# A hybrid attention and retention layer: a second pause in the index search, and later splits of the attention projection's weights

## The chip, the cores and the metric

The kernel runs on one core of one Trainium2 chip. The metric is the device time of one execution in microseconds (us); lower is better. Before the change it is 1831.25 us, the median of three runs (1830.81 to 1835.08). The engines are TensorE (PE), VectorE (DVE), ScalarE (ACT), GpSimd (POOL) and SyncE (SP), whose queue issues the DMAs.

## The reference

One decoder layer over a sequence of 1024 tokens, with model width 1024. What matters here:

```python
proj = jnp.dot(h, w_in)      # q, k, v; index q, k, w; retention q, k, v, g; two gates
# index scores: which keys a query may see
s_h = jnp.einsum('bqhd,bsd->bqhs', iqb, ikf) * idx_scale
score = jnp.einsum('bqh,bqhs->bqs', iwb * w_scale, jax.nn.relu(s_h))
score = jnp.where(causal[None], score, NEG)
_, idx = lax.top_k(score, topk)                  # topk = 256
# attention over the chosen keys, then
y_a = jnp.dot(att.reshape(B, S, N_HEADS_A * HEAD_DIM_A), w_attn_proj)
y_r = jnp.dot(jax.nn.silu(gr) * _head_groupnorm(ret, gn_w), w_ret_proj)
merged = jax.nn.sigmoid(ga) * y_a + jax.nn.sigmoid(gb) * y_r
x = x + gate1 * jnp.dot(merged, w_out)           # then a SwiGLU feed-forward and a norm
```

## The kernel before, in words

All matrix products of weights are done in three parts: a weight is split into a rounded part `hi` and a remainder `lo`, so is the activation, and hi·hi, hi·lo and lo·hi are summed in a bank of PSUM. The split of a weight (`split_weight`, L70, and `split_block`, L704) is one copy on ACT and one subtraction on POOL.

The stages that matter follow each other on PE like this:

1. Projections, index scores and retention (to about 490 us).
2. **Gated projections** (`run`, from L996): the remaining columns of `w_in`, multiplied by a Strassen-Winograd scheme with seven products for a 2x2 block (`Stream`, L708). For each product DVE may form a sum of weight blocks (`factor`, L739 and L743, into `wraw`), ACT and POOL split it (L706, L707), PE multiplies it (L771 to L775), ACT copies a result out of PSUM (L754) or DVE adds to one (L757, into `kept`, `sums`, `spare`).
3. **Retention tiles** (`make_g`, L932): eight tiles for each half of the tokens are transposed, gated on DVE (L936) and split (hi on ACT, L938; lo on DVE, L939).
4. **Retention projection** (from L996): y_r for eight column blocks `nt`. The first three are done half by half, with the last eight `make_g` between them; blocks 3 to 7 take both halves at once in two PSUM banks. DVE multiplies each result by its gate (`y_r_store`, L988, `sgr`).
5. **Attention** (from L1115): four pairs of heads `p`, eight blocks of 128 queries `qb`, two heads `e`, so 64 tiles. For each tile PE makes the logits (`lga`), DVE adds the mask and takes the maximum, ACT takes the exponential (L1060, `sx`), POOL scales (L1062), PE transposes (`tra`, three tiles behind the logits), ACT or DVE copies the result (`pt`, L1077, L1079), and PE multiplies with the values (`pva`). Blocks 2 to 7 of the queries use the finished index scores as the mask.
6. **Attention projection** (from L1162), its eight weight slots loaded and split by `cols_slot` (L101), and then the output projection, whose weights POOL multiplies by a gate (L1257) before they are split.

The **index search** (`select_all`, L436) finds for each query the 256th largest score by bisection on the bits of the float. For each bit from 30 to 0 DVE counts, in each of six score blocks (384 to 1024 columns), how many scores lie above the candidate (L450, a compare that also accumulates), then two tiny steps set the bit (L455, L470). A last count and five steps a block (L478 to L482) turn the scores into a mask. All of it is DVE work, issued with a late priority, so that the scheduler puts it between the other instructions. A scheduler sets the order in each engine's queue when the program is built; at run time each engine takes its queue strictly in that order. `turns_after` adds a dependency that only orders two instructions in one queue. With one, bit 8's first count stands behind the last split of the token sums in stage 2 (`paused[0]`).

PSUM has eight banks. In stages 2 to 4 they are three `mm`, two `tr` and three `lg`. Buffers for raw weights `wraw` are four by the time of the attention projection's loads: load 5 needs the buffer that the split of load 1 frees, and so on, and the loads of the output projection follow in the same ring.

Of the kernel before, what the change touches and what calls it, by code (L numbers as in the profile page):

```python
# [14 lines left out]
AF = mybir.ActivationFunctionType  # L15
# [4 lines left out]
P = 128  # L20
# [4 lines left out]
H = 512  # L25
HD = 64
# [17 lines left out]
def tile_hybrid_layer(ctx: ExitStack, tc: tile.TileContext, x, c, w_ada, b_ada, norm1_w, w_in,  # L44
                      w_attn_proj, w_ret_proj, gn_w, w_out, norm2_w, w_ffn_gate, w_ffn_up,
                      w_ffn_down, final_norm_w, rope_r, rope_a, rope_c, ret_mask, ret_scale, causal, out):
    nc = tc.nc
# [17 lines left out]
    def f32(ap):  # L65
        return ap.bitcast(F32)

    RING = 11

    def split_weight(raw, n, order=None, home=None):  # L70
        if home is not None:
            hi, lo = home[:, 0], home[:, 1]
        else:
            hi = ring.tile([P, H], R, name="whi", tag="whi", bufs=RING)
            lo = ring.tile([P, H], R, name="wlo", tag="wlo", bufs=RING)
        if order is None:
            nc.scalar.activation(hi[:, :n], raw[:, :n], AF.Copy)  # L77
            nc.gpsimd.tensor_sub(lo[:, :n], raw[:, :n], f32(hi[:, :n]))  # L78
        else:
            raw, hv, lv = order(raw, hi, lo)  # L80
            nc.scalar.activation(hv, raw, AF.Copy)
            nc.gpsimd.tensor_sub(lv, raw, f32(hv))
        return hi, lo
# [14 lines left out]
            nc.gpsimd.tensor_mul(raw[:, :n], raw[:, :n], scale)  # L98
        return split_weight(raw, n)

    def cols_slot(w, kt0, c0):  # L101

        raw = raw_tile()
        nc.sync.dma_start(
            out=raw.rearrange("p (k n) -> p k n", k=4),
            in_=w[kt0 * P:(kt0 + 4) * P, c0:c0 + P].rearrange("(k p) n -> p k n", p=P))
        return split_weight(raw, H)

    def mm_tok(ps, lhs, slots, n=H, ks=None):

# [11 lines left out]
    def turns_after(ins, other):  # L122

        tc.add_manual_dep(ins.ins, other.ins.name, NOSYNC, reason="order")
# [75 lines left out]
    def ps_mm():  # L200
        return psx.tile([P, H], F32, name="mm", tag="mm", bufs=3)
# [4 lines left out]
    def ps_lg():  # L206
        return psx.tile([P, H], F32, name="lg", tag="lg", bufs=3)
# [216 lines left out]
        last_score[0] = nc.vector.tensor_add(sc[:, W - P:W], sc[:, W - P:W], cm01[:, P:2 * P])  # L424

    last_score = [None]
    PAUSE = 8
    paused = []

    def all_scores():  # L430
# [5 lines left out]
    def select_all():  # L436

        tc.cur_priority += LATE
        n = len(score)
        cand, rej = (early.tile([P, 8], I32, name=x)[:, :n] for x in ("cand", "rej"))
        cnt, need = (early.tile([P, 8], F32, name=x)[:, :n] for x in ("cnt", "need"))
        eq = early.tile([P, S], U8, name="eq")
        rank = early.tile([P, S], I16, name="rank")
        at = [cand.bitcast(F32)[:, j:j + 1] for j in range(n)]

        def count(op, thr):
            ins = [nc.vector.tensor_scalar(eq[:, :sc.shape[1]], sc, thr[j], None, op0=op, op1=ALU.add,  # L450
                                           accum_out=cnt[:, j:j + 1]) for j, sc in enumerate(score)]
            return ins[0]

        def rejected(value):
            nc.vector.tensor_scalar(rej, cnt, float(TOPK), float(value), op0=ALU.is_lt, op1=ALU.mult)  # L455


        for j, sc in enumerate(score):
            ins = nc.vector.tensor_scalar(eq[:, :sc.shape[1]], sc, 0.0, None, op0=ALU.is_ge, op1=ALU.add,
                                          accum_out=cnt[:, j:j + 1])  # L460
            tc.add_manual_dep(ins.ins, last_score[0].ins.name, NOSYNC, reason="scores first")
        rejected(-1)
        nc.vector.tensor_scalar(cand, rej, 1 << 30, None, op0=ALU.bitwise_xor)
        for bit in range(30, -1, -1):
            first = count(ALU.is_ge, at)
            if bit == PAUSE:
                paused.append(first)
            rejected(1 << bit)
            if bit:
                nc.vector.scalar_tensor_tensor(cand, cand, 1 << (bit - 1), rej, op0=ALU.bitwise_xor,  # L470
                                               op1=ALU.bitwise_xor)
            else:
                nc.vector.tensor_tensor(cand, cand, rej, op=ALU.bitwise_xor)
        count(ALU.is_gt, at)
        nc.vector.tensor_scalar(need, cnt, -1.0, float(TOPK), op0=ALU.mult, op1=ALU.add)
        for j, sc in enumerate(score):
            e, r = eq[:, :sc.shape[1]], rank[:, :sc.shape[1]]
            nc.vector.tensor_scalar(e, sc, at[j], None, op0=ALU.is_equal)  # L478
            nc.vector.tensor_tensor_scan(r, e, e, 0.0, op0=ALU.add, op1=ALU.max)
            nc.vector.scalar_tensor_tensor(e, r, need[:, j:j + 1], e, op0=ALU.is_gt, op1=ALU.mult)  # L480
            nc.vector.tensor_scalar(sc, sc, at[j], NEG, op0=ALU.is_lt, op1=ALU.mult)
            nc.vector.scalar_tensor_tensor(sc, e, NEG, sc, op0=ALU.mult, op1=ALU.add)  # L482
        tc.cur_priority -= LATE
# [6 lines left out]
    for t in range(NT):  # L490
        ps = ps_mm()
        for k in range(KT):
            n = 5 * (KT * t + k) // 4 - 8
# [5 lines left out]
        st = projp.tile([P, H], F32, name="vst", bufs=2)  # L499
# [432 lines left out]
    def make_g(k, hf, rt, sg):  # L932
        tp = ps_tr()
        for i in range(4):
            nc.tensor.transpose(tp[:, i * P:(i + 1) * P], rt[:, i * P:(i + 1) * P], ident)
        nc.vector.scalar_tensor_tensor(sg, tp, colT[:, 72 + k:73 + k], sg, op0=ALU.mult, op1=ALU.mult)  # L936
        hi = gT.hi[hf][:, k, :]
        nc.scalar.activation(hi, sg, AF.Copy)  # L938
        nc.vector.tensor_sub(gT.lo[hf][:, k, :], sg, f32(hi))  # L939


    seq = [(st, m) for m in ORDER for st in flow[:2]]
# [54 lines left out]
    for hf in range(2):  # L997
        for nt in range(NF):
            slots, sg = first[nt]
            ps = ps_mm()  # L1000
            mm_ch([ps], gT, slots, (hf,))
            y_r_store(hf, ps, sg)
            if hf == 0:
                for k in ((0, 1, 2), (3, 4, 5), (6, 7))[nt]:
                    make_g(k, 1, *staged[k])
            else:
                nc.sync.dma_start(out=m_d[nt], in_=sg)
    st_s.close()
    pre = pool("pre", side="left", stack=mid)
    for nt in range(NF, KT):  # L1010
        slots, sg = y_r_open(nt)
        pss = [ps_mm(), ps_mm()]
        mm_ch(pss, gT, slots)
        for hf in range(2):
            y_r_store(hf, pss[hf], sg)
        nc.sync.dma_start(out=m_d[nt], in_=sg)
        if nt in (4, 5):
            make_stack(nt - 4, pre)
# [15 lines left out]
        nc.sync.dma_start(out=v, in_=v_d[:, :, p * P:(p + 1) * P])  # L1034
        return v

    def att_logits(qb, st):
        qs, kh, kl = st
        W = (qb + 1) * P
        sx = att.tile([P, S], F32, name="sx", bufs=6)  # L1040
        mx = att.tile([P, 16], F32, name="mx", bufs=6)
        if qb < 2:
            bias = cm01[:, P:2 * P] if qb == 0 else cm01
        else:
            bias = score[qb - 2]
        chunks = {1: (256,), 2: (256,), 3: (384,), 4: (512,), 5: (384, 256), 6: (512, 256), 7: (512, 384),
                  8: (512, 512)}[qb + 1]
        c0 = 0
        for i, n in enumerate(chunks):
            lg = psa.tile([P, H], F32, name="lga", bufs=4)  # L1050
            nc.tensor.matmul(lg[:, :n], lhsT=qs[:, qb * P:(qb + 1) * P], rhs=kh[:, c0:c0 + n], start=True, stop=False)
            nc.tensor.matmul(lg[:, :n], lhsT=qs[:, qb * P:(qb + 1) * P], rhs=kl[:, c0:c0 + n], start=False, stop=True)
            n = min(n, W)
            nc.vector.tensor_tensor_reduce(
                out=sx[:, c0:c0 + n], in0=lg[:, :n], in1=bias[:, c0:c0 + n], op0=ALU.add, op1=ALU.max, scale=1.0,
                scalar=-3e38 if i == 0 else mx[:, i - 1:i], accum_out=mx[:, i:i + 1])
            c0 += n
        top = mx[:, len(chunks) - 1:len(chunks)]
        nc.vector.tensor_scalar(mx[:, 2:3], top, -(HD ** -0.5), None, op0=ALU.mult)
        nc.scalar.activation(sx[:, :W], sx[:, :W], AF.Exp, scale=HD ** -0.5, bias=mx[:, 2:3], accum_out=mx[:, 3:4])  # L1060
        nc.vector.reciprocal(mx[:, 3:4], mx[:, 3:4])  # L1061
        nc.gpsimd.tensor_scalar(sx[:, :W], sx[:, :W], mx[:, 3:4], 1.0, op0=ALU.mult, op1=ALU.mult)  # L1062
        return sx
# [51 lines left out]
    for p in range(4):  # L1115
        for qb in range(NT):
            for e in range(2):
                sx = att_logits(qb, stacks[2 * p + e])
                todo_t.append((p, qb, e, sx))
                drain(3, 1)  # L1120
            if p < 3 and qb == 0:
                v_sb[p + 1] = load_v(p + 1)
                for h in (2 * p + 2, 2 * p + 3):
                    make_stack(h, pre if p == 1 else att)
# [35 lines left out]

    sg5 = slab_tile(6, [P, 4, S], F32, "sg5")
    for nt in range(KT):  # L1162
        slot = cols_slot(w_attn_proj, 0, nt * P)
        sg = sg5[:, nt % 4, :]
        nc.sync.dma_start(out=sg, in_=sga_d[nt])
        for hf in range(2):
# [481 lines left out]
```

## Time and profile before

| what | value |
|---|---|
| median of three runs | 1831.25 us |
| the profiled execution's own time | 1836.64 us |
| its span, first to last instruction | 1834.9 us |
| PE busy | 1712.6 us (93%) |
| DVE busy | 1222.0 us (67%) |
| POOL busy | 937.4 us (51%) |
| ACT busy | 739.8 us (40%) |
| mean granted TensorE clock | 0.982 |
| DMA | 266.49 MB, mean 145 GB/s |

The profile is of one execution. Its page gives busy shares and groups of instructions by source line; its trace can be asked for stretches of time, for waits (who waited for whom, by semaphores), and for single instructions in order of time. A wait is put down to the instruction that came last, even where that one was itself only held up by another. Some matmul records are missing, so counts of matmuls are a little low.

### The profile page before, as it was taken

The page shows a single profiled execution, that of the slowest core. Times are in us where ns is not written, and L with a number is a line of the kernel's source. Part 1 is how long each engine was busy: PE and PEld are TensorE (multiplying, and loading weights), DVE is VectorE, ACT ScalarE, POOL GpSimd, SP SyncE. Part 2 cuts the span into 40 slices and gives each one's busy share as a digit, 9 for nine tenths or more (in the row PEclk, how much of TensorE's full clock was granted, in tenths as well). Part 3 has the DMA queues.
Part 4 walks back from the last instruction along what each step waited for, and adds up shares of the span by engine and source line. Part 5 has one row for each costly group of instructions (what it writes and reads, how often), then busy time and mean ns, then how long its engine had stood idle before and what let it go on. Part 6 is the DMA issues. An engine that isn't in the chain of part 4 may idle for free. (4 is left out here: it accounts for less than half of the span.)

```text
span 1834.9 us, 24613 instructions
## 1 busy us (share of the span) xinstructions
PE 1712.6 (93%) x8266; PEld 1399.1 (76%) x8266; DVE 1222.0 (67%) x2088; ACT 739.8 (40%) x1448; POOL 937.4 (51%) x902
## 2 busy tenths in 40 slices
PE   5899989999989979999989999889998999999998
PEld 3788868878768758788767888677776788788887
DVE  7637599999699995441557547765666555377565
ACT  3525532432443324430567235443332333355444
POOL 4571293773553669530454634444444444466564
PEclk9999999999989999999989999999999999999999
DMA  8530245433323335874851730134666333287663
GB/s 287 162 83 34 75 138 172 136 94 115 110 81 115 107 104 194 251 217 143 204 141 49 230 136 24 53 97 165 231 218 244 113 120 98 94 262 233 188 177 113
DMA packets 184703, 266.49 MB, mean 145 GB/s; under 512 B 13872, under 2 KB 113664, under 8 KB 182144
## 3 DMA queue, kind: packets, MB, share of 16 engines
q1 hardware_dynamic: 184576, 264.91, 46.3%
q8 instruction: 65, 1.06, 0.3%
q14 instruction: 62, 0.51, 0.1%
HBM read 195.39 MB, written 69.47 MB: 144 GB/s over the span
## 5 line engine op out<-in xcount | busy, mean ns | idle before, releaser
L707 POOL TENSOR_TENSOR flo<-tmp,fhi 128x512 fp32r<-128x512 f32 x88 | 129.2, 1470 | 157.5 <-ACT fhi L706 127.6
L78 POOL TENSOR_TENSOR wlo<-wraw,whi 128x512 fp32r<-128x512 f32 (+2 forms) x116 | 142.3, 1239 | 104.7 <-ACT whi L77 99.3
L450 DVE TENSOR_SCALAR_CACHE_REDUCE eq<-score,cand 128x384 uint8<-128x384 f32 (+2 forms) x192 | 180.7, 941 | 4.2
L116 PE MATMUL mm<-whi,hT_hi 128*128 128x512 f32 (+1 forms) x432 | 162.5, 379 | 2.3 <-ACT qk L611 1.8
L119 PE MATMUL mm<-whi,hT_lo 128*128 128x512 f32 (+1 forms) x432 | 163.2, 379 | 0.0
L118 PE MATMUL mm<-wlo,hT_hi 128*128 128x512 f32 (+1 forms) x432 | 162.8, 377 | 0.0
L771 PE MATMUL ya<-hc,fhi 128*128 128x512 f32 x336 | 134.8, 402 | 14.9 <-DVE c L757 13.5
L1496 DVE TENSOR_TENSOR dslot<-draw,dslot 128x512 fp32r<-128x512 f32 x88 | 93.8, 1093 | 70.6 <-ACT dslot L1495 62.4
L773 PE MATMUL ya<-hc,fhi 128*128 128x512 f32 x336 | 134.0, 399 | 5.2 <-DVE hc L1415 5.2
L775 PE MATMUL ya<-hc,flo 128*128 128x512 f32 x336 | 132.3, 398 | 0.0
L1495 ACT ACTIVATE dslot<-draw 128x512 fp32r<-128x512 f32 x154 | 90.2, 626 | 97.1 <-PE ya L1514 37.3
L1496 POOL TENSOR_TENSOR dslot<-draw,dslot 128x512 fp32r<-128x512 f32 x66 | 97.4, 1485 | 62.1 <-ACT dslot L1495 59.4
L77 ACT ACTIVATE whi<-wraw 128x512 fp32r<-128x512 f32 (+2 forms) x116 | 66.9, 591 | 129.6 <-DMA wraw<-in_w_in_dram 53.1
L707 POOL TENSOR_TENSOR flo<-raws,fhi 128x512 fp32r<-128x512 f32 x58 | 80.7, 1392 | 73.8 <-ACT fhi L706 57.0
L771 PE MATMUL yb<-hc,fhi 128*128 128x512 f32 x248 | 97.8, 395 | 5.5 <-ACT hc L1414 3.7
L706 ACT ACTIVATE fhi<-tmp 128x512 fp32r<-128x512 f32 x88 | 55.3, 632 | 117.4 <-PE ya L773 72.7
L775 PE MATMUL yb<-hc,flo 128*128 128x512 f32 x248 | 96.8, 391 | 3.2 <-POOL flo L707 3.2
L707 POOL TENSOR_TENSOR wlo<-wraw,whi 128x512 fp32r<-128x512 f32 x52 | 83.6, 1615 | 30.9 <-ACT whi L706 25.1
L773 PE MATMUL yb<-hc,fhi 128*128 128x512 f32 x248 | 96.8, 390 | 1.8 <-DVE hc L1415 1.7
L1062 POOL TENSOR_SCALAR sx<-sx,mx 128x1024 f32<-128x1024 f32 (+7 forms) x64 | 47.4, 748 | 98.7 <-DVE mx L1061 74.1
L116 PEld LDWEIGHTS mm<-whi,hT_hi 128*128 128x128 f32 x432 | 82.2, 191 | 14.5 <-ACT qk L611 2.2
L119 PEld LDWEIGHTS mm<-whi,hT_lo 128*128 128x128 f32 x432 | 82.3, 191 | 12.7
(400 smaller groups left out, 4951.1 us busy)
## 6 DMA issues: line engine op xcount, KB each, us to landing
draw<-act_d SPq DMA_DIRECT2D x77, 256.0 KB
mw<-in_w_ada_dram SPq DMA_DIRECT2D x32, 512.0 KB
act_d<-c SPq DMA_DIRECT2D x62, 256.0 KB
raw<-in_w_in_dram SPq DMA_DIRECT2D x26, 512.0 KB
raws<-in_w_ffn_gate_dram SPq DMA_DIRECT2D x24, 512.0 KB
raws<-in_w_ffn_up_dram SPq DMA_DIRECT2D x24, 512.0 KB
dw<-in_w_ffn_down_dram SPq DMA_DIRECT2D x22, 512.0 KB
dw_d<-dw SPq DMA_DIRECT2D x11, 1024.0 KB
```

Of the source, the lines that this page charges most:

```text
L77: nc.scalar.activation(hi[:, :n], raw[:, :n], AF.Copy)
L78: nc.gpsimd.tensor_sub(lo[:, :n], raw[:, :n], f32(hi[:, :n]))
L116: ins = nc.tensor.matmul(ps, lhsT=ahi, rhs=whi[:, :n], start=(i == 0), stop=False)
L118: nc.tensor.matmul(ps, lhsT=ahi, rhs=wlo[:, :n], start=False, stop=False)
L119: nc.tensor.matmul(ps, lhsT=alo, rhs=whi[:, :n], start=False, stop=(i == last))
L450: ins = [nc.vector.tensor_scalar(eq[:, :sc.shape[1]], sc, thr[j], None, op0=op, op1=ALU.add, accum_out=cnt[:, j:j + 1]) for j, sc in enume ...
L707: nc.gpsimd.tensor_sub(lo, src, f32(hi))
L771: mm = nc.tensor.matmul(ps, lhsT=whi[:, k, :], rhs=hhi[:, k, :], start=first, stop=False, skip_group_check=True)
L773: nc.tensor.matmul(ps, lhsT=whi[:, k, :], rhs=hlo[:, k, :], start=False, stop=False, skip_group_check=True)
L775: nc.tensor.matmul(ps, lhsT=wlo[:, k, :], rhs=hhi[:, k, :], start=False, stop=last, skip_group_check=True)
L1495: nc.scalar.activation(slot[:, 0], raw, AF.Copy)
L1496: lo_eng.tensor_sub(slot[:, 1], raw, f32(slot[:, 0]))
```

## The change

Four edits:

- The search gets a second pause: the first count of bit 3 must stand behind `made`, the last `gT_lo` of stage 3. `make_g` now returns that instruction. Bits 3 to 0, the final count and the masks move behind it.
- In the retention projection blocks 3 to 7 use one `mm` and one `lg` bank each, where they used two `mm`.
- The ACT half of the split of the attention projection's weight `nt` must stand behind the exponential of the second head in pair `2 + nt // 4`, query block `2 * (nt % 4)`.
- `att_logits` takes `p`, to note the exponentials under `exps[p, qb]`.

```diff
-    def split_weight(raw, n, order=None, home=None):
+    def split_weight(raw, n, order=None, home=None, behind=None):
...
-            nc.scalar.activation(hi[:, :n], raw[:, :n], AF.Copy)
+            ins = nc.scalar.activation(hi[:, :n], raw[:, :n], AF.Copy)
+            if behind is not None:
+                turns_after(ins, behind)
             nc.gpsimd.tensor_sub(lo[:, :n], raw[:, :n], f32(hi[:, :n]))
...
-    PAUSE = 8
+    PAUSES = (8, 3)
...
-            if bit == PAUSE:
+            if bit in PAUSES:
                 paused.append(first)
...
-        nc.vector.tensor_sub(gT.lo[hf][:, k, :], sg, f32(hi))
+        return nc.vector.tensor_sub(gT.lo[hf][:, k, :], sg, f32(hi))
...
-                    make_g(k, 1, *staged[k])
+                    made = make_g(k, 1, *staged[k])
...
+    turns_after(paused[1], made)
...
-        pss = [ps_mm(), ps_mm()]
+        pss = [ps_mm(), ps_lg()]
...
-        nc.scalar.activation(sx[:, :W], sx[:, :W], AF.Exp, scale=HD ** -0.5, bias=mx[:, 2:3], accum_out=mx[:, 3:4])
+        exps[p, qb] = nc.scalar.activation(sx[:, :W], sx[:, :W], AF.Exp, scale=HD ** -0.5, bias=mx[:, 2:3],
+                                           accum_out=mx[:, 3:4])
...
-        slot = cols_slot(w_attn_proj, 0, nt * P)
+        slot = cols_slot(w_attn_proj, 0, nt * P, exps[2 + nt // 4, 2 * (nt % 4)])
```

`cols_slot` only hands `behind` on to `split_weight`. In the changed kernel lines after the first edits have higher numbers (L450 becomes L454, L757 becomes L761, L988 becomes L992, L1054 becomes L1061, L1060 becomes L1067).

The order of DVE's instructions before, where bit 3 follows bit 4 in the gated projections (`eq`, `cnt` and `cand` are the search's, `score_768` is the block of 384 columns, the rest are the gated streams' additions):

```order
L455 TENSOR_SCALAR rej<-cnt 128x6
L470 SCALAR_TENSOR_TENSOR cand<-cand,rej 128x6
L450 TENSOR_SCALAR eq,cnt<-score_768,cand 128x384
L757 TENSOR_TENSOR kept<-kept,lg 128x512
L450 TENSOR_SCALAR eq,cnt<-score_769,cand 128x512
L450 TENSOR_SCALAR eq,cnt<-score_770,cand 128x640
L450 TENSOR_SCALAR eq,cnt<-score_771,cand 128x768
L757 TENSOR_TENSOR spare<-spare,mm 128x512
```

The same place in the changed kernel:

```order
L459 TENSOR_SCALAR rej<-cnt 128x6
L474 SCALAR_TENSOR_TENSOR cand<-cand,rej 128x6
L761 TENSOR_TENSOR kept<-kept,lg 128x512
L761 TENSOR_TENSOR spare<-spare,mm 128x512
L761 TENSOR_TENSOR kept<-kept,lg 128x512
L761 TENSOR_TENSOR sums<-sums,lg 128x512
L761 TENSOR_TENSOR sums<-sums,mm 128x512
```

After bit 4 only the streams' own additions and factor sums are left on DVE until the retention tiles are done.

DVE's order before at the end of the retention projection, up to attention's first instructions (`gT_lo` is the last gated tile, `sgr` the retention products):

```order
L939 TENSOR_TENSOR gT_lo_7304<-stage,gT_hi_7303 128x512 x2
L988 TENSOR_TENSOR sgr<-mm,sgr 128x512 x13
L1054 ISA sx,mx<-lga,cm_774 128x128
L1054 ISA mx 128x1
L1054 ISA sx,mx<-lga,cm_774 128x128
```

In the changed kernel the same place begins with the last gated tile and bit 3:

```order
L943 TENSOR_TENSOR gT_lo_7304<-stage,gT_hi_7303 128x512 x2
L454 TENSOR_SCALAR eq,cnt<-score_768,cand 128x384
L454 TENSOR_SCALAR eq,cnt<-score_769,cand 128x512
L454 TENSOR_SCALAR eq,cnt<-score_770,cand 128x640
L454 TENSOR_SCALAR eq,cnt<-score_771,cand 128x768
L454 TENSOR_SCALAR eq,cnt<-score_772,cand 128x896
L992 TENSOR_TENSOR sgr<-mm,sgr 128x512
```

and ends with the last block's mask, the last pair of products and attention:

```order
L486 SCALAR_TENSOR_TENSOR score_772<-eq,score_772 128x896
L482 TENSOR_SCALAR eq<-score_773,cand 128x1024
L483 SCALAR_TENSOR_TENSOR rank<-eq 128x1024
L485 TENSOR_SCALAR score_773<-score_773,cand 128x1024
L484 SCALAR_TENSOR_TENSOR eq<-rank,need,eq 128x1024
L486 SCALAR_TENSOR_TENSOR score_773<-eq,score_773 128x1024
L992 TENSOR_TENSOR sgr<-mm,sgr 128x512
L992 TENSOR_TENSOR sgr<-lg,sgr 128x512
L1061 ISA sx,mx<-lga,cm_774 128x128
```

So the rest of the search, with the thirteen products spread through it, stands between the last gated tile and attention.

POOL's order before, in the second head pair (L78 is a split's remainder, L1062 scales the exponentials `sx`, L1257 multiplies the output projection's first weight tiles, `wraw_10020` and the next, by the gate):

```order
L78 TENSOR_TENSOR wlo_9846<-wraw_9843,whi_9845 128x512
L78 TENSOR_TENSOR wlo_9885<-wraw_9882,whi_9884 128x512
L78 TENSOR_TENSOR wlo_9924<-wraw_9921,whi_9923 128x512
L78 TENSOR_TENSOR wlo_9963<-wraw_9960,whi_9962 128x512
L1257 TENSOR_TENSOR wraw_10020<-wraw_10020,gate1_9999 128x512
L1062 TENSOR_SCALAR sx_8469<-sx_8469,mx_8470 128x384
L1257 TENSOR_TENSOR wraw_10025<-wraw_10025,gate1_9999 128x512
```

On POOL in the last head pair of the changed kernel the same instructions stand between the scalings:

```order
L1070 TENSOR_SCALAR sx_9203<-sx_9203,mx_9204 128x128
L80 TENSOR_TENSOR wlo_9846<-wraw_9843,whi_9845 128x512
L1070 TENSOR_SCALAR sx_9241<-sx_9241,mx_9242 128x256
L1265 TENSOR_TENSOR wraw_10020<-wraw_10020,gate1_9999 128x512
L1070 TENSOR_SCALAR sx_9265<-sx_9265,mx_9266 128x256
L1070 TENSOR_SCALAR sx_9297<-sx_9297,mx_9298 128x384
L80 TENSOR_TENSOR wlo_9885<-wraw_9882,whi_9884 128x512
```

So the last four splits and the first multiplications move from the second head pair into the last one, each multiplication with scalings of the softmax right behind it.

More of the change, by code (lines that the diff above doesn't have):

```diff
@@ L99, in rows_slot, with cols_slot @@
         return split_weight(raw, n)
-    def cols_slot(w, kt0, c0):
+    def cols_slot(w, kt0, c0, behind=None):
         raw = raw_tile()
@@ L106, in cols_slot @@
             in_=w[kt0 * P:(kt0 + 4) * P, c0:c0 + P].rearrange("(k p) n -> p k n", p=P))
-        return split_weight(raw, H)
+        return split_weight(raw, H, behind=behind)
     def mm_tok(ps, lhs, slots, n=H, ks=None):
@@ L1035, in load_v, with att_logits @@
         return v
-    def att_logits(qb, st):
+    exps = {}
+    def att_logits(p, qb, st):
         qs, kh, kl = st
@@ L1117, in tile_hybrid_layer @@
             for e in range(2):
-                sx = att_logits(qb, stacks[2 * p + e])
+                sx = att_logits(p, qb, stacks[2 * p + e])
                 todo_t.append((p, qb, e, sx))
```

## The prediction

> **What bounds the kernel now.** I read the stretches of the program first, then who kept TensorE (PE) waiting in each, then the engines behind those waits. The table of windows has, after the window's length, the busy time and instruction count of PE, its weight loads, VectorE (DVE), ScalarE (ACT) and GpSimd (POOL), the granted TensorE clock, the DMA share and GB/s. The five rows are: gated projections while the search runs beyond bit 4; gated projections and the start of the retention tiles without any search; the rest of the retention projection; attention, first and second part.
>
> ```profile
> 588.00:680.50 92.50, 75.80 (x313) 58.84 (x312) 91.17 (x121) 28.83 (x52) 52.07 (x33) 0.96 0.33 100
> 681.00:762.00 81.00, 78.61 (x344) 64.03 (x343) 41.38 (x36) 38.02 (x67) 69.03 (x49) 1.00 0.61 192
> 816.50:882.00 65.50, 65.19 (x290) 53.87 (x288) 8.21 (x14) 2.53 (x4) 5.13 (x4) 1.00 0.51 148
> 882.00:945.00 63.00, 52.87 (x407) 40.49 (x408) 38.21 (x171) 40.60 (x98) 36.31 (x42) 0.92 0.82 192
> 945.00:1015.00 70.00, 70.00 (x650) 55.85 (x651) 46.17 (x191) 46.99 (x112) 25.95 (x34) 1.00 0.35 103
> ```
>
> PE is the bound everywhere except in two of these rows. In 588 to 680.5 DVE is full (91.17 of 92.5 us) and PE idles 16.7 us; in 882 to 945 PE idles 10.1 us with no engine full. In 816.5 to 882 DVE has only 8.21 us of work in 65.5. The waits of PE in the first row's window (us in total, times, longest):
>
> ```profile
> PE mm L775 <- POOL wlo L707: 5.2, 3, 2.3
> PE lg L771 <- ACT sums L754: 5.0, 1, 5.0
> PE lg L771 <- ACT whi L706: 2.1, 1, 2.1
> PE mm L771 <- DVE sums L757: 1.5, 1, 1.5
> PE mm L771 <- ACT kept L754: 1.4, 1, 1.4
> PE mm L771 <- ACT whi L706: 1.0, 2, 0.7
> PE lg L775 <- POOL wlo L707: 0.4, 1, 0.4
> ```
>
> They name POOL and ACT, but neither is full (52 and 29 us of 92.5): both stand behind factor sums (L739, L743) and additions (L757) that DVE does between search instructions. Without the search, in 681 to 762, PE waits far less:
>
> ```profile
> PE mm L771 <- DVE sums L757: 1.8, 1, 1.8
> PE lg L771 <- ACT whi L706: 0.3, 1, 0.3
> PE lg L771 <- ACT kept L754: 0.3, 1, 0.3
> ```
>
> In attention the largest PE wait is for ACT's copies of transposed tiles, and ACT itself waits, ahead of the split of the attention projection's weights, for their DMA (first PE's row, then ACT's):
>
> ```profile
> PE pva L1094 <- ACT pt L1079: 8.4, 2, 7.0
> ```
>
> ```profile
> ACT whi L77 <- DMA wraw<-in_w_attn_proj_dram: 10.2, 4, 6.8
> ```
>
> After a long wait PE also restarts at half clock; the two stretches behind the 5.0 and the 7.0 us wait, same columns as above:
>
> ```profile
> 646.30:650.30 4.00, 3.99 (x9) 3.18 (x10) 3.96 (x5) 0.44 (x1) 1.86 (x1) 0.50 0.45 130
> 924.60:930.30 5.70, 5.70 (x38) 4.81 (x39) 1.68 (x6) 3.58 (x11) 5.55 (x6) 0.50 0.29 89
> ```
>
> **Part 1: the search leaves the gated projections from bit 3 on.** Bits 8 to 4 stay; the order shows bit 3 and all that follows behind the last retention tile. Of PE's 16.6 us of waits (5.2+5.0+2.1+1.5+1.4+1.0+0.4) I leave the 2.4 us (1.8+0.3+0.3) that the stretch without search shows. The half clock cost 4.0 × 0.5 = 2.0 us. So this part gives 16.6 + 2.0 − 2.4 = **16.2 us**. It could be 18.6 (no wait left) or less if POOL is next: 33 instructions took it 52.07 us there, but these were drawn out beside the search, and in the second row it does 49 in 69.03 of 81 us while PE runs on.
>
> **Part 2: where the search goes.** It starts after the last gated tile (first row below) and all of it stands on DVE ahead of attention's first instruction, while the last retention product now ends on the second row. A bit of the search, alone on DVE, takes 6.34 us (third fence, DVE 6.06 us in 14 instructions).
>
> ```profile
> 815.15 1.35 DVE L939 TENSOR_TENSOR gT_lo<-stage,gT_hi 128x512 fp32r<-128x512 f32 x2
> ...
> 881.02 1.29 DVE L988 TENSOR_TENSOR sgr<-mm,sgr 128x512 f32<-128x512 f32 x2 [9.59 <-PE mm L133]
> ```
>
> ```profile
> 595.33:601.67 6.34, 6.34 (x30) 5.25 (x29) 6.06 (x14) 1.20 (x2) 0.00 (x0) 1.00 0.12 44
> ```
>
> Bits 3 to 0 and the final count are five passes: 31.7 us. Then each of six score blocks is masked in five steps. Groups (with mean ns of one) in their present place, and the block of 768 columns:
>
> ```profile
> L479 DVE TENSOR_TENSOR_SCAN rank<-eq 128x384 int16<-128x384 uint8 (+5 forms) x6 | 13.1, 2186 | 0.2
> L480 DVE SCALAR_TENSOR_TENSOR eq<-rank,need,eq 128x384 uint8<-128x384 int16 (+5 forms) x6 | 7.7, 1280 | 0.0
> L482 DVE SCALAR_TENSOR_TENSOR score<-eq,score 128x384 f32<-128x384 uint8 (+5 forms) x6 | 7.3, 1222 | 0.1
> L481 DVE TENSOR_SCALAR score<-score,cand 128x384 f32<-128x384 f32 (+5 forms) x6 | 7.3, 1209 | 0.0
> L478 DVE TENSOR_SCALAR eq<-score,cand 128x384 uint8<-128x384 f32 (+5 forms) x6 | 6.5, 1077 | 0.1
> ```
>
> ```profile
> 650.69 0.61 DVE L478 TENSOR_SCALAR eq<-score,cand 128x768 uint8<-128x768 f32 x1
> 651.34 1.76 DVE L479 TENSOR_TENSOR_SCAN rank<-eq 128x768 int16<-128x768 uint8 x1
> 653.01 0.59 DVE L481 TENSOR_SCALAR score<-score,cand 128x768 f32<-128x768 f32 x1
> 653.52 0.68 DVE L743 TENSOR_TENSOR wraw<-raw,raw 128x512 f32<-128x512 f32 x1
> 654.12 1.01 DVE L480 SCALAR_TENSOR_TENSOR eq<-rank,need,eq 128x768 uint8<-128x768 int16 x1
> 655.05 0.68 DVE L757 TENSOR_TENSOR sums<-sums,lg 128x512 f32<-128x512 f32 x1
> 655.65 0.95 DVE L482 SCALAR_TENSOR_TENSOR score<-eq,score 128x768 f32<-128x768 uint8 x1
> ```
>
> The groups sum to 41.9 us. This block takes 0.61+1.76+0.59+1.01+0.95 = 4.92 us, 6.4 ns a column, which for all 4224 columns is 27.1 us. The difference is POOL: the block ran in a pause of POOL's splits. In the new place POOL has almost nothing to do:
>
> ```profile
> 833.97 1.29 POOL L78 TENSOR_TENSOR wlo<-wraw,whi 128x512 fp32r<-128x512 f32 x1 [9.30 <-ACT whi L77]
> 884.95 0.38 POOL L1062 TENSOR_SCALAR sx<-sx,mx 128x128 f32<-128x128 f32 x1 [49.70 <-DVE mx L1061]
> ```
>
> So I take 27.1. [...]
>
> The retention products between take three of about 0.7 us (half of 1.29) and five pairs of 1.29: 8.5 us; for pairs that aren't ready yet I add 1.5 us, an estimate. Search and products fill 31.7 + 27.1 + 8.5 + 1.5 = 68.8 us from 816.5, to 885.3. Now DVE is free for attention at 882.3. **Late by 3 us**; with masks at 41.9 late by 17.8, and not late at all if the estimate of 1.5 and the pairs' overlap are too high. PE can put only four logit tiles ahead of that. PE doesn't wait for the retention products meanwhile: tiles now alternate between two groups of three banks (mm, lg), and a pair takes PE about 10.9 us (9.59 + 1.29), more than DVE is ever behind; so I cost that edit at nothing. With only the three mm banks a pair left waiting would have held PE. The few neighbours that change places on ACT in the gated projections I cost at nothing too: ACT is busy for 29 of 92.5 us there.
>
> **Part 3: the splits in attention.** The first four weights still load early; ACT reaches a split only behind exponentials of the third and fourth head pair, where the data is long there. PE gets back 8.4 us and 5.7 × 0.5 = 2.9 us of clock: **11.3 us**. In exchange the last 70 us, where PE is full, get eight splits: on ACT of 0.6 us each (page: below), on POOL of 1.29, and four multiplications of w_out by the gate.
>
> ```profile
> L77 ACT ACTIVATE whi<-wraw 128x512 fp32r<-128x512 f32 (+2 forms) x116 | 66.9, 591 | 129.6 <-DMA wraw<-in_w_in_dram 53.1
> ```
>
> ACT has 47 and POOL 26 of 70 us there, so the bulk hides; transposes run three tiles behind the logits. What may not hide: on SyncE's queue the loads 5 to 8 and the four of w_out each wait for a buffer that a split frees, and POOL's multiplication stands ahead of softmax scalings. Before, that cost POOL 0.68 us once:
>
> ```profile
> 934.07 2.54 POOL L1257 TENSOR_TENSOR wraw<-wraw,gate 128x512 f32<-128x512 f32 x2 [0.68 <-DMA wraw<-in_w_out_dram]
> ```
>
> I put **2 us** on it (three of four such waits exposed), from 0 to 11 (all of the gain). Behind them on SyncE stand only the last values tile, needed a head pair later, and the projection's inputs, whose space comes free at attention's end anyway.
>
> **The sum.** −16.2 + 3 − 11.3 + 2 = −22.5 us. The profiled execution took 1836.64 us (span 1834.9 and 1.7 around it), so it would be 1814; it lies 5.4 us over the median of 1831.25, from which I predict **1809 us**. The rest is PE-bound and only shifts.
>
> **Rivals.**
> *Masks at the old price* (41.9): for it, that is what they cost; against it, POOL is idle. 1809 + 14.8 = 1824.
> *Attention gives it back*: splits and POOL's waits stall the full second part for 11.3 more: 1820. Against it, the cover of three tiles, about 6 us (133 us of attention over 64 tiles).
> *The late start opens a half-clock stretch*: as behind 7.0 us, 2.9 us, so 1812. [...]
> *POOL becomes the bound of the gated projections*, half of part 1 stays: 1817.
> *Slower*: POOL's four multiplications block as ACT did, 7.0 + 2.9 us each: 1809 − 2 + 39.6 = 1847. It decides from 6.1 us a block (24.5 over four). Against it, DMA is only 0.35 busy there, against 0.82 where ACT waited.
> *The search is only moved*: old mask price and attention's gain lost together: 1835, no change.
>
> **Chances.** Forecast 0.51 (its own range 1803 to 1815); masks 0.14; half clock 0.12; attention gives back 0.10; POOL 0.07; only moved 0.03; slower 0.03. About 0.3% (5.5 us) is what a measurement can tell from no change: faster 0.94, same 0.03, slower 0.03. The range reaches down to 1801 (no late start, no new waits, no wait left: 1809 − 7.4) and up to 1821, past the rivals at 1820 and short of the one at 1824.
>
> **What would show it.** Right: PE's waits between bit 4 and the retention tiles fall to 2 or 3 us and that window shortens by 16; five masks of 768 columns sum to near 4.9 us; DVE's first attention instruction comes about 69 us after the last gated tile (now 65.8); ACT's wait for w_attn_proj is gone. Wrong: POOL or ACT full in the gated window, a PE gap of 10 us or more at attention's start, or PE waiting for POOL's scalings in the last head pair.

## The result and the profile after

| | before | changed |
|---|---|---|
| median, first four runs of each | 1831.03 us (1830.06 to 1835.08) | 1805.03 us (1802.61 to 1810.25) |
| ratio | | 0.9842, 95% interval 0.9818 to 0.9866 |
| profiled execution, span | 1834.9 us | 1802.3 us |
| PE busy | 1712.6 us (93%) | 1706.0 us (95%) |
| DVE busy | 1222.0 us | 1212.2 us |
| mean granted TensorE clock | 0.982 | 0.988 |

The medians differ by 26.0 us, the two profiled executions by 32.6. To see where that is, I took the start of the same matmuls in both traces and subtracted (the median of nine neighbours, at points named by their time before). The changed kernel is 2.9 us behind at 588, 19.2 ahead at 684, 19.9 at 815, only 16.8 at 884, 27.0 at 1013 and 1180, and 32.6 at 1450. So the gated projections beyond bit 4 gave 22.0 us, the start of attention took 3.1, and attention gave 10.2. The last 5.6 us are in the feed-forward, which the change doesn't touch; every other kernel below shows 2 to 5 us there too, against the same execution of before, so most of this belongs to that execution.

The windows of the changed kernel, in the columns of the prediction: gated projections beyond bit 4 (590 to 661), the stretch behind it, the last gated tile to attention's first DVE work, attention's two parts.

```profile
590.00:661.00 71.00, 71.00 (x315) 58.80 (x314) 25.35 (x25) 29.50 (x52) 45.18 (x33) 1.00 0.43 130
661.00:743.00 82.00, 80.38 (x355) 65.58 (x354) 42.10 (x37) 39.03 (x69) 68.47 (x50) 1.00 0.61 195
796.60:864.70 68.10, 65.36 (x291) 54.04 (x290) 64.31 (x112) 2.54 (x4) 5.13 (x4) 1.00 0.53 152
864.70:920.00 55.30, 55.08 (x447) 43.25 (x446) 40.85 (x189) 41.15 (x101) 24.95 (x35) 0.97 0.80 184
920.00:988.00 68.00, 67.52 (x611) 52.62 (x612) 42.40 (x173) 47.00 (x109) 37.39 (x42) 1.00 0.38 110
```

The first row is 71 us where 92.5 stood, with PE busy in all of it and DVE in a third. The third shows DVE nearly full (64.31 of 68.1 us), and PE idle for 2.7 us. The fourth has no idle PE, but a clock of 0.97.

DVE from the last gated tile to attention's first work, with the masks of the block of 768 columns between:

```profile
795.90 0.69 DVE L943 TENSOR_TENSOR gT_lo<-stage,gT_hi 128x512 fp32r<-128x512 f32 x1
...
845.95 0.62 DVE L482 TENSOR_SCALAR eq<-score,cand 128x768 uint8<-128x768 f32 x1
846.60 1.76 DVE L483 TENSOR_TENSOR_SCAN rank<-eq 128x768 int16<-128x768 uint8 x1
848.28 0.59 DVE L485 TENSOR_SCALAR score<-score,cand 128x768 f32<-128x768 f32 x1
848.79 1.01 DVE L484 SCALAR_TENSOR_TENSOR eq<-rank,need,eq 128x768 uint8<-128x768 int16 x1
849.83 0.96 DVE L486 SCALAR_TENSOR_TENSOR score<-eq,score 128x768 f32<-128x768 uint8 x1
...
864.74 0.28 DVE L1061 CUSTOM_DVE_ANT_0 sx<-lga,cm 128x128 f32<-128x128 f32 x1
```

From 796.59 to 864.74 are 68.15 us. All the masks together, by group:

```profile
L483 DVE TENSOR_TENSOR_SCAN rank<-eq 128x384 int16<-128x384 uint8 (+5 forms) x6 | 9.7, 1623 | 0.2
L484 DVE SCALAR_TENSOR_TENSOR eq<-rank,need,eq 128x384 uint8<-128x384 int16 (+5 forms) x6 | 5.7, 944 | 0.0
L486 DVE SCALAR_TENSOR_TENSOR score<-eq,score 128x384 f32<-128x384 uint8 (+5 forms) x6 | 5.3, 890 | 0.2
L482 DVE TENSOR_SCALAR eq<-score,cand 128x384 uint8<-128x384 f32 (+5 forms) x6 | 3.5, 586 | 0.2
L485 DVE TENSOR_SCALAR score<-score,cand 128x384 f32<-128x384 f32 (+5 forms) x6 | 3.4, 561 | 0.0
```

They sum to 27.6 us where they took 41.9. Who holds PE at attention's start, in order of time, and the stretch behind it as a window:

```profile
860.91 0.40 PE L137 MATMUL lg<-gT_hi,wlo 128*128 128x512 f32 x1
861.14 0.28 PE L1058 MATMUL lga<-kk,qs 128*128 128x256 f32 x1
861.26 0.28 PE L1059 MATMUL lga<-kk,qs 128*128 128x256 f32 x1
864.28 0.39 PE L1058 MATMUL lga<-kk,qs 128*128 128x256 f32 x1 [2.74 <-DVE sgr L992]
```

```profile
864.70:868.10 3.40, 3.40 (x13) 3.11 (x12) 2.90 (x22) 2.71 (x8) 0.42 (x2) 0.50 0.96 236
```

PE makes two logit matmuls, then waits 2.7 us for DVE's last product, and behind that wait the clock stands at half for 3.4 us. All that PE waits for after that, to the end of attention:

```profile
PE tra L1081 <- DVE pt L1085: 0.5, 1, 0.5
PE lga L1058 <- DVE mx L1061: 0.2, 1, 0.2
```

Neither the wait for `pt` of 8.4 us nor ACT's for the attention projection's weights is left. On POOL, in the last 68 us of attention, the splits and the multiplications of the output projection's weights (least, median and greatest ns; first and last start):

```profile
L80 POOL TENSOR_TENSOR wlo<-wraw,whi x8: 1266/1278/1300, 919.5 to 975.2; 128x512 fp32r<-128x512 f32 x8
L1265 POOL TENSOR_TENSOR wraw<-wraw,gate x4: 1265/1280/1297, 955.0 to 979.7; 128x512 f32<-128x512 f32 x4
```

No multiplication waited for a DMA there; one did later, in the attention projection (6.9 us before 1000.4), and PE waited for nothing then. SyncE's queue waited 30 us for the buffers of these loads, and no PE wait came of it:

```profile
SPq L1264 <- POOL wlo L80: 30.0, 4, 9.6
```

### The profile page after: what moved, and what is told of

It reads as the page before. It is cut to its first block, busy times and chain, and to the rows that moved or that the text cites. A ratio compares the mean times of both kernels' runs of the same rounds, so it can differ in the third digit from the quotient of the medians.

```text
span 1802.3 us, 24616 instructions
## 1 busy us (share of the span) xinstructions
PE 1706.0 (95%) x8266; PEld 1397.9 (78%) x8266; DVE 1212.2 (67%) x2088; ACT 740.5 (41%) x1448; POOL 937.9 (52%) x902
## 5 line engine op out<-in xcount | busy, mean ns | idle before, releaser
L454 DVE TENSOR_SCALAR_CACHE_REDUCE eq<-score,cand 128x384 uint8<-128x384 f32 (+2 forms) x192 | 180.8, 942 | 4.3
L775 PE MATMUL ya<-hc,fhi 128*128 128x512 f32 x336 | 133.7, 399 | 12.1 <-DVE c L761 10.2
L1070 POOL TENSOR_SCALAR sx<-sx,mx 128x128 f32<-128x128 f32 (+7 forms) x64 | 47.5, 747 | 92.1 <-DVE mx L1069 69.2
L711 POOL TENSOR_TENSOR wlo<-wraw,whi 128x512 fp32r<-128x512 f32 x52 | 79.8, 1544 | 29.0 <-ACT whi L710 24.6
```

Of the source, the lines that this page charges most:

```text
L711: nc.gpsimd.tensor_sub(lo, src, f32(hi))
L775: mm = nc.tensor.matmul(ps, lhsT=whi[:, k, :], rhs=hhi[:, k, :], start=first, stop=False, skip_group_check=True)
```

## The experiments

The theory was that two independent parts add up: the gated projections lose the search's waits, less a late start of attention, and attention loses ACT's wait for weights. Totals of one kernel's runs lie up to 17 us apart (the kernel before, 1825.5 to 1842.3), so each kernel is read by its stages as above, and by its total only for a check. Gains are negative, in us against the profiled execution of before; another choice of neighbouring matmuls moves single columns by up to 0.4 us. Stages that a kernel leaves as they were come out within 0.8 us of before (splits only in the first three columns, counts for masks in the third and fourth), but for the second column, which is less steady. Each ratio is against runs of the kernel before made beside that row's own.

| kernel | 588 to 684 | 684 to 815 | 815 to 884 | 884 to 1013 | sum to 1180 | median us | ratio (95%) |
|---|---|---|---|---|---|---|---|
| changed | -22.0 | -0.8 | +3.1 | -10.2 | -29.9 | 1805.0 | 0.9842 (0.9818 to 0.9866) |
| pause only | -22.0 | +2.5 | +3.2 | -5.0 | -21.3 | 1810.2 | 0.9879 (0.9861 to 0.9897) |
| splits only | -0.1 | -0.5 | 0 | -9.0 | -9.6 | 1824.5 | 0.9956 (0.9943 to 0.9968) |
| three mm banks | -22.0 | -0.5 | +3.0 | -10.2 | -29.7 | 1801.7 | 0.9834 (0.9812 to 0.9856) |
| pause at bit 2 | -22.0 | -0.7 | 0 | -9.5 | -32.2 | 1804.1 | 0.984 (0.982 to 0.9859) |
| pause at the masks | -19.8 | -0.3 | 0 | -8.8 | -28.9 | 1802.8 | 0.9838 (0.9813 to 0.9863) |
| counts for masks | -17.9 | +2.9 | 0 | -0.8 | -15.8 | 1818.9 | 0.9928 (0.99 to 0.9956) |
| splits one pair earlier | -22.0 | -0.7 | +3.1 | -9.6 | -29.2 | 1803.8 | 0.9846 (0.9821 to 0.987) |
| splits in the last pair | -22.0 | +2.4 | +2.4 | -10.9 | -28.0 | 1802.3 | 0.9832 (0.9807 to 0.9858) |
| bit 2 and last pair | -22.0 | +2.3 | 0 | -10.0 | -29.7 | 1799.5 | 0.9821 (0.9793 to 0.9848) |
| changed, again | -22.0 | -0.3 | +3.1 | -10.2 | -29.4 | 1806.3 | 0.9856 (0.983 to 0.9883) |

The column 684 to 815 holds a PE wait for one DVE addition near 730, of 1.0 us in the changed kernel and 2.6 to 2.8 in the three rows with +2.3 to +2.5. In these three the clock also stood at half for 3.4 us behind it. The wait's size changes from execution to execution, for code that is the same; the +2.9 of the counts has no such stretch of half clock, and its cause stays open.

**Pause only.** The diffs below are against the changed kernel, where nothing else is said.

```diff
-        slot = cols_slot(w_attn_proj, 0, nt * P, exps[2 + nt // 4, 2 * (nt % 4)])
+        slot = cols_slot(w_attn_proj, 0, nt * P)
```

> The pause at bit 3 and the mm and lg banks alone; the attention projection's weights are split where they were before. Theory (two parts that add up): the gated projections lose their waits (22 to 23 us) and attention starts 2.9 us late, so 1831 - 20 = 1811 to 1814, with ACT's wait of about 10 us for w_attn_proj and PE's 7 us wait for pt back in the first head pair. Rival (the pause alone brings everything, the late splits nothing): 1805, with no PE wait over 3 us in attention. Second rival (the late start of attention hides ACT's wait, because PE would have waited for DVE at that time): 1808.

The gated projections show the whole gain. In attention PE's and ACT's waits are back, but shorter (PE's rows, then ACT's):

```profile
PE pva L1102 <- ACT pt L1087: 4.9, 1, 4.9
PE lga L1058 <- DVE sgr L992: 2.7, 1, 2.7
```

```profile
ACT whi L77 <- DMA wraw<-in_w_attn_proj_dram: 5.8, 3, 4.7
```

ACT waits 5.8 us for the weights where it waited 10.2, and attention gains 5.0 us even without the late splits, which makes good its late start of 3.2. So the second rival holds in part: a late start runs alongside the DMA that ACT would have waited for. The first rival falls, as PE waits 4.9 us for `pt` again and attention gains 5.2 us less than in the changed kernel.

**Splits only.**

```diff
-    PAUSES = (8, 3)
+    PAUSES = (8,)
...
-    turns_after(paused[1], made)
...
-        pss = [ps_mm(), ps_lg()]
+        pss = [ps_mm(), ps_mm()]
```

> The late splits alone, with the search paused only at bit 8 as before. Theory: attention gains 8.4 us of PE waits and 2.9 us of half clock less 0 to 2 us, so 1831 - 10 = 1821; the gated projections keep 16 us of PE waits. Rival (the splits in the first pair only filled time in which PE would have waited anyway): 1829 to 1832. Second rival (POOL's multiplications of w_out block the softmax in the last pair): 1825 or above, with PE waits behind POOL's scalings.

The windows of the gated projections and of attention's first part, same columns:

```profile
588.00:680.50 92.50, 77.14 (x318) 59.88 (x316) 91.13 (x127) 27.96 (x50) 50.47 (x32) 0.96 0.33 100
882.50:945.00 62.50, 60.57 (x505) 46.84 (x505) 43.89 (x200) 44.78 (x110) 26.95 (x38) 1.00 0.85 194
```

The first row is that of before; in the second PE has 505 matmuls in the time that held 407. Attention gains 9.0 us and no wait of PE is over 0.8 us, so the splits stand on their own. But the two parts don't simply add up. From 815 to 1013 the pause alone gives 1.8 us and the splits alone 9.0, and together they give 7.1: the late start already hides part of ACT's wait, so beside the pause the late splits are worth some 5 us. That the totals of the parts, 21.3 and 9.6, come to 30.9 where the change has 29.9 is luck, as the pause-only execution lost about 3 us more near 730.

**Three mm banks.**

```diff
-        pss = [ps_mm(), ps_lg()]
+        pss = [ps_mm(), ps_mm()]
```

> The changed kernel, but blocks 3 to 7 of the retention projection take two of the three mm banks again instead of one mm and one lg. Theory: DVE reads a finished pair up to about 2 us late, and the next pair of products needs a bank of the one before, so PE waits once a pair: 3 to 8 us more than the changed kernel, 1808 to 1813. Rival (the bank edit does nothing, as the first half of the next pair runs in the free third bank): 1805, no PE wait in the retention projection.

My theory fell. All of PE's waits from the last gated tile to attention's start:

```profile
PE lga L1058 <- DVE sgr L992: 2.7, 1, 2.7
```

There is none in the retention projection. The bank edit does nothing here.

**Pause at bit 2.**

```diff
-    PAUSES = (8, 3)
+    PAUSES = (8, 2)
```

> The changed kernel with the second pause at bit 2 instead of 3: one more bit of the search (about 6.3 us of DVE) runs in the gated projections, and the rest ends 6.8 us earlier, ahead of attention's first logits. Theory: attention's 2.7 us wait for DVE and its half clock (3.4 us at 0.5) go, 2.9 to 4.4 us; bit 3 among the gated streams costs at most the 1.4 us that PE waited in the first 20 us behind bit 4 before the change: 1801 to 1803. Rival (each us of search among the gated streams costs what it did on average before, 22 us in 92.5): 2.2 us back, 1803 to 1805. Second rival (the late start costs nothing, as attention is bound later): 1805 to 1807.

Bit 3 back among the gated streams costs nothing (22.0 again), and attention's late start is gone, with its half clock; the sum of the stages is 2.3 us better than the changed kernel's. The total is 1804.1, and the intervals can't tell it from the changed kernel.

**Pause at the masks.** Here only the masks move; bits 3 to 0 and the last count stay.

```diff
-    PAUSES = (8, 3)
+    PAUSES = (8,)
...
-            nc.vector.tensor_scalar(e, sc, at[j], None, op0=ALU.is_equal)
+            first = nc.vector.tensor_scalar(e, sc, at[j], None, op0=ALU.is_equal)
+            if j == 0:
+                paused.append(first)
```

> The changed kernel with the second pause ahead of the first mask step instead of bit 3: bits 3 to 0 and the last count stay in the gated projections, only the masks (27.6 us of DVE) go behind the last retention tile. Theory (the masks made all but 1.7 us of the 22 us that the search cost the gated projections, for in the trace of before PE falls back 1.7 us over the counts of bits 3 to 0 and 20 over the masks): the gated projections from bit 4 on keep 20 to 22 us of gain, attention starts with no wait for DVE, 1801 to 1803. Rival (search work costs by its DVE time, of which the counts are 40 of 92 us): about 10 us of the gain lost, 1811 to 1815.

All of PE's waits in the gated projections beyond bit 4:

```profile
PE mm L781 <- POOL wlo L713: 1.2, 1, 1.2
PE mm L777 <- ACT whi L712: 0.3, 1, 0.3
```

Five passes of counts, about two fifths of the search's DVE time there (31.7 us to the masks' 41.9), cost 2.2 of the 22.0 us; the masks cost the other 19.8. The same can be read from the trace of before, cut where the masks begin:

```profile
588.00:629.00 41.00, 39.49 (x173) 31.90 (x172) 40.01 (x81) 14.59 (x26) 17.12 (x13) 1.00 0.33 103
629.00:680.50 51.50, 36.31 (x142) 26.94 (x141) 51.15 (x41) 14.24 (x26) 34.96 (x21) 0.93 0.34 97
```

DVE is full in both rows, but PE loses 1.5 us in the first and 15.2 in the second, where its clock falls too. How the longest wait there, PE's 5.0 us for ACT's copy of `sums`, came about can be followed back: ACT's queue stood 6.9 us for a factor sum of DVE, which stood behind mask steps in DVE's queue and itself took 1.75 us:

```profile
641.80 1.63 DVE L482 SCALAR_TENSOR_TENSOR score<-eq,score 128x512 f32<-128x512 uint8 x1
643.36 1.75 DVE L739 TENSOR_TENSOR wraw<-raw,wraw 128x512 f32<-128x512 f32 x1
645.14 0.63 ACT L706 ACTIVATE whi<-wraw 128x512 fp32r<-128x512 f32 x1 [6.91 <-DVE wraw L739]
646.31 0.80 PE L771 MATMUL lg<-S,whi 128*128 128x512 f32 x1 [5.03 <-ACT sums L754]
```

**Counts for masks.** The kernel before; attention's mask is left out, and each block's five mask steps become five counts of the same block.

```diff
-            nc.vector.tensor_scalar(e, sc, at[j], None, op0=ALU.is_equal)
...
-            nc.vector.scalar_tensor_tensor(sc, e, NEG, sc, op0=ALU.mult, op1=ALU.add)
+            for _ in range(5):
+                nc.vector.tensor_scalar(e, sc, at[j], None, op0=ALU.is_ge, op1=ALU.add, accum_out=cnt[:, j:j + 1])
```

> The kernel before, but the five mask steps of each score block are replaced by five counts of the same block (so the attention mask is left out: attention adds raw scores). Five counts take 30.5 us of DVE alone, the masks 27.6 alone and 41.9 where they stood. Theory (the masks and POOL's splits slow each other, 14 us on DVE and about 0.5 us on each of 20 splits on POOL, and counts don't): the window between bit 4 and the search's end shortens by about 12 us, the groups of counts keep their price and POOL's splits stay at 1.3 to 1.4 us: 1816 to 1822. Rival (the order leaves the streams too few places on DVE, whatever the search's steps are): the window keeps its length within 3 us, 1828 to 1834.

POOL's split remainders beside the masks, in the kernel before:

```profile
L707 POOL TENSOR_TENSOR wlo<-wraw,whi 128x512 fp32r<-128x512 f32 x7 | 13.9, 1981 | 1.3 <-ACT whi L706 1.3
L707 POOL TENSOR_TENSOR wlo<-raw,whi 128x512 fp32r<-128x512 f32 x6 | 9.8, 1640 | 0.0
L707 POOL TENSOR_TENSOR wlo<-sums,whi 128x512 fp32r<-128x512 f32 x4 | 7.4, 1857 | 13.2 <-ACT whi L706 13.2
```

The same groups beside the counts, and below them the thirty counts on DVE:

```profile
L704 POOL TENSOR_TENSOR wlo<-wraw,whi 128x512 fp32r<-128x512 f32 x8 | 11.7, 1466 | 0.0
L704 POOL TENSOR_TENSOR wlo<-raw,whi 128x512 fp32r<-128x512 f32 x7 | 9.9, 1418 | 0.0
L704 POOL TENSOR_TENSOR wlo<-sums,whi 128x512 fp32r<-128x512 f32 x4 | 5.2, 1295 | 6.9 <-ACT whi L703 6.9
```

```profile
L479 DVE TENSOR_SCALAR_CACHE_REDUCE eq<-score,cand 128x384 uint8<-128x384 f32 (+5 forms) x30 | 28.2, 941 | 0.6
```

Counts with accumulator reads (30 of 0.08 us) take as long as the masks alone, 30.6 to 27.6 us, in the same place. Yet 17.9 of the 22.0 us are gone: more than my 12, and the rival (the window keeps its length) falls. The stretch with most of the counts, as a window:

```profile
632.00:665.50 33.50, 32.16 (x141) 25.97 (x140) 32.86 (x63) 14.49 (x26) 26.61 (x21) 1.00 0.50 149
```

DVE is as full as before, and PE loses 1.3 us where it lost 15.2. So it wasn't that DVE was full: masks and POOL's splits slow each other, the masks by half (41.9 us where they stood, 27.6 away from the splits) and the splits by 0.2 to 0.6 us each, and the streams wait for both. What else there is in the 17.9 beside the 11.3 us less on DVE (41.9 to 30.6) wasn't taken apart; nor was it tested whether a mask step such as the scan, 2.2 us in one piece on average, holds the streams up more than the shorter counts for its length alone. And 2.9 us are lost again by 815, so the masks' price over that of counts is 15 to 18 us.

**Splits one pair earlier, and all in the last pair.**

```diff
-        slot = cols_slot(w_attn_proj, 0, nt * P, exps[2 + nt // 4, 2 * (nt % 4)])
+        slot = cols_slot(w_attn_proj, 0, nt * P, exps[1 + nt // 4, 2 * (nt % 4)])
```

> The changed kernel with the first four splits in the second head pair and the last four in the third, one pair earlier. Theory (ACT waited for the weights' DMA in the first pair, and the data is there by the second): attention keeps its gain, 1803 to 1807, no ACT wait for w_attn_proj over 1 us. Rival (the splits need the last pairs, where PE is full and the other engines have slack): part of the 10 us comes back, 1808 to 1815, with PE waits for pt in the second pair.

Attention keeps 9.6 us. One row of it tests the slower rival of the prediction: POOL's multiplication did wait for its DMA here.

```profile
930.24 1.28 POOL L1265 TENSOR_TENSOR wraw<-wraw,gate 128x512 f32<-128x512 f32 x1 [5.83 <-DMA wraw<-in_w_out_dram]
936.52 1.27 POOL L1265 TENSOR_TENSOR wraw<-wraw,gate 128x512 f32<-128x512 f32 x1 [1.95 <-DMA wraw<-in_w_out_dram]
```

No wait of PE over 0.5 us followed, so here the three tiles between logits and transposes covered a POOL that was blocked for 5.8 us. The other placing had `exps[3, nt]` in this place:

> The changed kernel with all eight splits in the last head pair, one behind each block of queries. Theory (POOL's multiplications of w_out are no danger where their data comes in time; here the loads of w_out come some 20 us later and the multiplications fall into the attention projection, which has nothing on POOL): 1804 to 1810. Rival (the mechanism of the slower case: loads, splits and multiplications pile up in the last 30 us of attention and POOL or ACT block the softmax): PE waits of 6 us or more in the last pair or ahead of the attention projection, 1812 to 1830.

PE has no wait over 0.6 us in the last pair, and attention gains 10.9 us. The place of the splits is free from the second pair on; only the first pair, where the data wasn't there, was wrong.

**The two best placings together, and the changed kernel again on the same chip.** The first has `PAUSES = (8, 2)` and `exps[3, nt]`.

> The two placings put together that stood best in the stages: the second pause at bit 2, and all eight splits in the last head pair. Theory (stage gains add: 22 us in the gated projections, no late start of attention, 9.5 us in attention): from the gated projections to the attention projection 31 to 32 us less than before, against 29.5 for the changed kernel; total 1799 to 1802, 2 us under the changed kernel in the same call, which single runs (5 us apart) need not show. Rival (with attention on time, the splits in the last pair are exposed): PE waits over 3 us in the last pair, total as the changed kernel or above.

> The changed kernel unaltered, beside the one above, for a direct comparison on one chip. Expected: 1803 to 1806, ratio to before 0.984; 2.7 us of PE wait at attention's start again, if that comes from DVE's fixed order and not from the one execution.

Medians of six runs are 1799.5 and 1806.3. The intervals still overlap, and the stages of the two profiled executions are within 0.3 us (the first lost 2.3 near 730). By the late start it should be about 2.4 us faster; that it is 7 isn't shown.

## Why the prediction was right, and where it was off

Forecast: 1809, 1801 to 1821, faster. Measured: 1805.0. The steps:

- **Gated projections, 16.2 us; measured 22.0**, in all eight profiled executions whose second pause is at bit 3 or 2. The waits did go with the search, and the term was mis-sized: 22.0 lies beyond the 18.6 that I allowed for no wait left. I summed PE's waits, took off a rest of 2.4 that doesn't exist (the changed window shows no wait), and left PE's busy time alone but for 2.0 of half clock. But 313 matmuls were busy for 75.80 us where 315 now take 71.00: 2.8 us more of lost time lay inside the "busy" of matmuls whose ends are modelled. The window's length for the same matmuls, 92.5 against 71, is the safer measure. POOL didn't become the bound: it was busy for 45.18 of the 71 us.
- **Why they waited.** The path was right: PE waited for ACT and POOL, and these for factor sums in DVE's queue. But I put it down to DVE being full, and only the masks' dearer price to POOL, and the runs showed the masks to be nearly all of it: counts that fill DVE as much cost 2 to 7 us, the masks 15 to 20. As the change moves both, the forecast couldn't go wrong by this; that is luck. The counts keep their price in both places: one takes 941 ns beside POOL's splits (counts for masks) and 945 in the new place. Why the masks pay beside the splits and the counts don't was not shown.
- **Masks, 27.1 us; measured 27.6. Search and products, 68.8; measured 68.15. Late start, 3; measured 3.1 by 884, with 2.4 left in the end** (attention as a whole gains 9.5 without a late start and 7.1 with it). The rival with masks at 41.9 falls. PE put one logit tile ahead of DVE's last product, not the four that I had.
- **Half clock at the late start.** I gave it 0.12, taking a wait of 3 us for too short, which no run had shown; it came, at 2.7 us of wait (the last section works out when it does). It changed the sum little: the run with all splits in the last pair had the same wait without half clock, and lost 2.4 us by 884 where the others lost 3.0 to 3.2.
- **The banks.** I costed the edit at nothing, which is right, and said that three banks would have held PE, which the run with three shows to be wrong.
- **Attention, 11.3 less 2; measured 10.2.** The 2 us for POOL's waits were not there. Nor were all of the 11.3: without a late start the late splits gave 8.8 to 10.0, and part of the 10.2 is attention catching up its late start. That the difference came out near is luck in part. The rivals that give the gain back or block POOL fall: a block of 5.8 us cost PE nothing, and none of the size from which the slower case decides (6.1) occurred.
- **The sum** of the stages is 29.9 where I had 22.5; the median fell by 26.0. The 3.9 us between the stages and the medians aren't traced, as only one execution of the kernel before was profiled; its own time lies 5.6 us over their median.

## What to carry to other kernels

When work in the gaps of a busy stage holds it up, ask which of its instructions do so, and look at how long the neighbours on the other engines take beside them: the counts of this search were nearly free where they stood, and the masks cost 15 to 20 us for 27.6 us of work. Move the part that collides to a stage where the other engine is idle (here from a window in which POOL was busy for 52.07 of 92.5 us to one with 5.13 of 68.1), and only as much of it as ends before the next stage needs the engine. And a copy that waits for a transfer belongs behind the point where the data is there: before, ACT stood 6.8 us ahead of one such copy, with a copy of `pt` behind it in its queue, for which PE waited 7.0 us; in the changed kernel neither wait is left.

## What the runs showed of the hardware

- A PE wait of 2.7 us can be followed by half clock for 3.4 us. Of the six profiled executions with that wait at attention's start five show it (one of them with a start at 866.1, the wait having ended at 865.0), and the one with all splits in the last pair shows none, at the same wait:

```profile
PE lga L1058 <- DVE sgr L992: 2.7, 1, 2.7
```

- The traces of all twelve profiled executions give the measure. Every stretch of one clock in them, but the last, lasts a multiple of 3.41 us (in the changed kernel 143.4, 3.4, 341.3, 3.4, 290.1 and so on), so I cut each execution into steps of 3.41 us along these stretches and took PE's idle time in each step of full clock (by the profile, in which the ends of matmuls are modelled). Half clock came next behind all 113 steps with more than 1.91 us idle, behind 9 of the 18 with 1.78 to 1.91 us, and behind 1 of the 5920 with less, which lies in the first 40 us. So in these executions somewhat over half of a step was enough, and a wait's length alone did not decide: at attention's start the 2.7 us left 2.3 to 2.7 us idle in one step five times, with half clock behind it, and the sixth time the edge of a step fell into the wait, with 1.6 us as the larger part, and no half clock came.

- Two mask steps with one input and no accumulator were slowed more than those with two: beside POOL's splits and without them they take 1077 and 586 ns (`eq<-score`) and 1209 and 561 (`score<-score`), against 1280 and 944 (`eq<-rank`), 1222 and 890 (`score<-eq`) and 2186 and 1623 for the scan.
